# Seven-product output projection of a hybrid block on Trainium2: one order of block products for both row halves, half-sized accumulating loads, and the mixer's signed copies on ScalarE's queue

## The chip, the cores and the metric

The program runs on one core of one Trainium2 chip. The metric is the device time of one execution in microseconds (us), as the median of several runs. The profile is one more execution of the same program, taken by the hardware profiler. Its times are us from the start of its span. PE is TensorE (matmuls; PEld is its weight loads), DVE is VectorE, ACT is ScalarE, POOL is GpSimd, SP is SyncE; a name with a q (ACTq, POOLq, SPq) is the engine's instruction queue where it starts DMAs.

## The reference

One transformer-like block on x of shape (1, 512, 2048) in float32. Two mixers run side by side on one input projection, their outputs are put together and multiplied by `w_out`, and an MLP with a hidden width of 8192 follows.

```python
h = rmsnorm(x, norm_mix_pre)
proj = h @ w_in                                # 2048 -> 1024 (pool) + 4 x 1024 (q, f, i, g)
y_pool = pool_mixer(proj[..., :1024], ...)     # per group: (trailing mean over 2, 4, 8 or 16 rows
                                               #  minus the row) @ pool_w[j] + pool_b[j], times a scale
y_hgrn = hgrn2_mixer(q, f_pre, i, g, ...)      # gated linear recurrence, 8 heads of 128
mix = concat([y_pool, y_hgrn]) @ w_out         # 2048 x 2048
x = x + rmsnorm(mix, norm_mix_post)
h = rmsnorm(x, norm_mlp_pre)
ff = square(relu(h @ w_mlp_in)) @ w_mlp_out    # 2048 -> 8192 -> 2048
x = x + rmsnorm(ff, norm_mlp_post)
```

## The kernel before

**Precision.** Every operand of a large product is kept as two parts, a high part (a cast to a shorter float, on ACT) and a low part (the remainder, a subtraction on DVE). A product is three matmuls on PE: high by high, high by low, low by high. PE therefore carries nearly the whole time, and ACT and DVE feed it with split operands: for each 1 MB of weights (128 x 2048) two casts on ACT (L1052) and two subtractions on DVE (L1053), each of half the block.

**The stages.** The input projection (L269) runs first, column group by column group, until about 542 us. Tasks of other work (the pool mixer, the recurrence) are put between its matmuls by a clock: `clock.tick()` stands after each block of the projection (12 matmuls on one PSUM bank), and a task that says `yield n` is taken up again n ticks later. Then comes the product with `w_out` ("the mix", slots m0 to m27), then the MLP's two products.

**The pool mixer's first half** (`pool_chunk(0)`, c = 0) runs in the second column group. It makes trailing sums on DVE, the difference (`diff`), the split of the difference into `dh` and `dl` (`split`: ACT L514, DVE L515; both live in a tile whose name in the trace is mx), and then `maps(g)`: for each of two output tiles six small matmuls (tile pps, L522 to L524) with the group's weights. There are two groups, g = 0 and 1, which share the rooms `dh` and `dl`.

**The signed copies.** Each mixer's finished 128 x 512 piece goes, with signs + and -, to DRAM (`mix_dram`): `stash` makes two scaled copies on ACT (L465, tile signed, which has two rooms) and starts one 256 KB DMA on POOL's queue (L467). There are 16 of them. The operand sums of the mix are read back from there (tile terms, `load_terms`, and `add_from_dram` L1202, which adds while it loads, on POOL's queue).

**The mix as seven products.** The product with `w_out` is done twice by a seven-product scheme for 2 x 2 blocks, once for each half of the contraction (e = 0, 1), and twice for the pairs of column blocks (n2 = 0, 1): 28 slots of 24 matmuls each (L1132). A slot (n2, i, e) uses product number i, `ORDER = (1, 2, 5, 3, 6, 7, 4)`. Products 1, 6, 7, 4 are summed in the PSUM banks oa, products 2, 5, 3 in the banks og. The weights of products 1, 5, 6, 4 lie in one room (`MXW[n2, e]`) and are made one from the other: when product 1's block has been split, an accumulating DMA on POOL's queue (L1079, 1 MB) adds another block of `w_out` to it in place, and the room holds the weights of product 5; likewise 5 to 6 and 6 to 4. Product 2 has a room of its own (`MY[n2, e]`), which is then loaded anew with the block from which product 3 and, by one accumulating load, product 7 come.

**What sets the order.** For each slot m the program is written in this sequence: the weighing of finished pieces on DVE (`run_weighs`, L1160), the split of slot m+1's weights (`mix_split_gen(m + 1)`, after which the next load or accumulation into that room is issued), the steps that a table `mplan[m]` puts ahead of the slot, the slot's 24 matmuls, and after each half (12 matmuls) the evacuation of its bank (`evac_half`: an ACT copy L1148, or a DVE add L1151 onto the row tile YL) and one clock tick. The second halves of `mplan`'s entries (amid) run after the first half's evacuation. All engines execute their own instructions in this order, so a step that waits holds what stands behind it on its engine. In the order before, the slots for n2 = 0 run through `ORDER` for e = 0 (m0 to m6), and for e = 1 as 2, 1, 5, 3, 6, 7, 4 (m7 to m13). The weights of slot m8 (product 1) go into a room that `late_pools()` opens only at m5 (`second_rooms`), named YZ; its load is an SP DMA.

**Start of the MLP.** Slots k0, k1, ... of a second table, `plan`, are the first MLP products; the steps `s1`, `s2`, `s3`, `s7` make the signed sums of its operand blocks on DVE, `spl` splits them (L913/L914 for weights, similar lines for these).

## Time and profile before

| | |
|---|---|
| time, median of 3 runs | 1947.95 us (1947.37 to 1949.28) |
| the profiled execution's own time | 1949.39 us |
| its span | 1947.7 us |
| mean granted TensorE clock | 0.992 |
| PE busy | 1910.2 us, 10816 matmuls |
| DVE, ACT, POOL busy | 1309.0, 887.3, 186.8 us |
| DMA | 376.61 MB, mean 193 GB/s |

The busy time of PE counts a matmul longer when the clock is granted at less than full speed, so a high share does not say that PE runs at its pace. In a list by time, a row reads: start (us), duration (us), engine, line, operation, out<-in, shape, count, and in brackets the idle time of the engine just before it with what ended that idle time. In a list of waits the columns are: waiting engine, tile and line, the releaser, total us, times, longest. In the table by stretches: the stretch, its length, the busy time of PE, PEld, DVE, ACT, POOL with the number of instructions in brackets, the granted PE clock (PEclk), the DMA share and GB/s.

### The profile page before, as it was taken

To read this page: it belongs to the slowest core of one execution; us is meant where nothing else is said; L and a number is where in the kernel's file an instruction comes from. 1 tells how busy PE (TensorE), PEld (TensorE's weight loads), DVE (VectorE), ACT (ScalarE), POOL (GpSimd) and SP (SyncE) were. 2 spreads that over 40 slices of the span, in tenths; PEclk is the share of its full clock that TensorE was granted. 3 is DMA by queue.
4 is the path that set the end of the run, shared out by engine and by line. 5 is a ranking of instruction groups with operands and counts; after the bars stand their busy time and mean duration, and the time that the engine had idled before them with its cause. 6 is when DMAs were issued, how large, how long until landed. Compare 5 with 4: busy or idle time off the path is not lost.

```text
span 1947.7 us, 26198 instructions
## 1 busy us (share of the span) xinstructions
PE 1910.2 (98%) x10816; PEld 1621.6 (83%) x10816; DVE 1309.0 (67%) x1370; ACT 887.3 (46%) x1063; POOL 186.8 (10%) x291
## 2 busy tenths in 40 slices
PE   9899999999979999999999999999999999999997
PEld 8788888888857899988888888888888888888886
DVE  5537346375557777566665766677778878878787
ACT  6321232213545676444444444446544444444455
POOL 3000000000110101101111111011010010010111
PEclk9999999999989999999999999999999999999999
DMA  8322223323578889988889789898897897897987
GB/s 314 109 87 88 87 92 112 110 88 139 136 204 240 215 232 218 229 235 198 218 218 218 219 217 211 236 236 243 208 248 221 201 236 229 215 222 207 235 215 148
DMA packets 61672, 376.61 MB, mean 193 GB/s; under 512 B 6768, under 2 KB 7792, under 8 KB 23408
## 3 DMA queue, kind: packets, MB, share of 16 engines
q0 software_dynamic: 28064, 176.70, 44.3%
q1 hardware_dynamic: 33344, 197.97, 28.1%
q8 instruction: 85, 1.39, 0.3%
q14 instruction: 35, 0.29, 0.0%
q10 hardware_dynamic: 144, 0.26, 0.0%
HBM read 345.54 MB, written 29.36 MB: 192 GB/s over the span
## 4 chain that ended last, share of the span: by engine, by line
PE 65%; DVE 2%; DMA 1%; ACT 1%; issue 1%; DVEq 0%; ACTq 0%
PE ps L1351 18%; PE al L1571 16%; PE ga L1571 12%; PE ps L1354 9%; PE oa L1132 2%; PE la L1571 2%; PE og L1366 2%; PE lg L1571 2%; PE og L1132 2%; DMA YZ<-in_w_mlp_in 1%; DVE ml L914 1%; PE oa L1366 1%; DVE ml L1053 1%; DMA X<-in_w_out 0%; DMA YZ<-in_w_out 0%
## 5 line engine op out<-in xcount | busy, mean ns | idle before, releaser
L1351 PE MATMUL ps<-a,mh 128*128 128x512 f32 x1536 | 370.6, 391 | 0.0
L1351 PEld LDWEIGHTS ps<-a,mh 128*128 128x128 f32 x1536 | 280.9, 188 | 53.7 <-issue 0.3
L1571 PE MATMUL al<-mh,o 128*128 128x512 f32 x896 | 277.2, 389 | 0.0
L913 ACT CAST mh<-X 128x1024 fp32r<-128x1024 f32 x176 | 180.5, 1055 | 206.4 <-PE ps L1351 82.9
L913 ACT CAST mh<-YX 128x1024 fp32r<-128x1024 f32 x176 | 180.6, 1055 | 159.1 <-PE al L1571 46.3
L914 DVE TENSOR_TENSOR ml<-X,mh 128x1024 fp32r<-128x1024 f32 x176 | 207.4, 1220 | 54.0 <-ACT mh L913 53.8
L269 PE MATMUL pj<-xT,wh 128*128 128x512 f32 x760 | 236.0, 392 | 0.0
L914 DVE TENSOR_TENSOR ml<-YX,mh 128x1024 fp32r<-128x1024 f32 x176 | 207.4, 1220 | 31.3 <-ACT mh L913 31.2
L1571 PE MATMUL ga<-mh,o 128*128 128x512 f32 x672 | 208.0, 389 | 0.0
L1354 PEld LDWEIGHTS ps<-a,ml 128*128 128x128 f32 x1536 | 199.6, 191 | 9.0
L1354 PE MATMUL ps<-a,ml 128*128 128x256 f32 x1536 | 202.4, 283 | 0.0
L1571 PEld LDWEIGHTS al<-mh,o 128*128 128x128 f32 x896 | 168.2, 188 | 35.0
L1571 PE MATMUL al<-ml,o 128*128 128x512 f32 x448 | 174.3, 389 | 0.0
L269 PEld LDWEIGHTS pj<-xT,wh 128*128 128x128 f32 x760 | 142.9, 189 | 29.7
L269 PE MATMUL pj<-wh,xT 128*128 128x512 f32 x512 | 164.7, 395 | 0.0
L228 ACT CAST wh<-wr 128x1024 fp32r<-128x1024 f32 (+1 forms) x84 | 82.5, 1007 | 180.3 <-PE pj L269 142.0
L229 DVE TENSOR_TENSOR wl<-wr,wh 128x1024 fp32r<-128x1024 f32 (+1 forms) x84 | 97.7, 1172 | 94.8 <-ACT wh L228 94.8
L913 ACT CAST mh<-YZ 128x1024 fp32r<-128x1024 f32 x96 | 98.6, 1053 | 127.4 <-PE ps L1351 50.6
L269 PE MATMUL pj<-xT,wl 128*128 128x512 f32 x380 | 148.5, 391 | 0.0
L1571 PEld LDWEIGHTS ga<-mh,o 128*128 128x128 f32 x672 | 126.1, 188 | 26.2
L1400 DVE TENSOR_TENSOR t<-t,ps 128x512 f32<-128x512 f32 x120 | 82.4, 687 | 88.4 <-ACT t L1403 67.2
L914 DVE TENSOR_TENSOR ml<-YZ,mh 128x1024 fp32r<-128x1024 f32 x96 | 113.1, 1220 | 34.4 <-ACT mh L913 34.4
(322 smaller groups left out, 2813.8 us busy)
## 6 DMA issues: line engine op xcount, KB each, us to landing
wr<-in_w_in SPq DMA_DIRECT2D x38, 1024.0 KB, 4.9
X<-in_w_mlp_in POOLq DMA_DIRECT2D x33, 1024.0 KB, 10.0
X<-in_w_mlp_out POOLq DMA_DIRECT2D x33, 1024.0 KB, 8.3
YX<-in_w_mlp_in POOLq DMA_DIRECT2D x23, 1024.0 KB, 9.9
YX<-in_w_mlp_out POOLq DMA_DIRECT2D x23, 1024.0 KB, 9.0
YX<-in_w_mlp_in SPq DMA_DIRECT2D x21, 1024.0 KB, 5.8
YX<-in_w_mlp_out SPq DMA_DIRECT2D x21, 1024.0 KB, 4.8
YZ<-in_w_mlp_in SPq DMA_DIRECT2D x16, 1024.0 KB, 9.0
```

Source lines behind the costliest of these rows:

```text
L228: nc.scalar.copy(out=hi[:, ks, :], in_=raw[:, ks, :])
L229: nc.vector.tensor_tensor(out=lo[:, ks, :], in0=raw[:, ks, :], in1=hi[:, ks, :].bitcast(F32), op=ALU.subtract)
L269: nc.tensor.matmul(bank, l, r, start=first and kt == 0 and oi == 0, stop=last and kt == 3 and oi == 2)
L913: nc.scalar.copy(out=hi[:, ks, :], in_=raw[:, ks, :])
L914: nc.vector.tensor_tensor(out=lo[:, ks, :], in0=raw[:, ks, :], in1=hi[:, ks, :].bitcast(F32), op=ALU.subtract)
L1053: nc.vector.tensor_tensor(out=lo[:, ks, :], in0=halves[h], in1=hi[:, ks, :].bitcast(F32), op=ALU.subtract)
L1132: nc.tensor.matmul(bank[h], l, r[:, kt, :], start=begins and kt == 0 and oi == 0, stop=ends_ and kt == 3 and oi == 2, skip_group_check=True)
L1351: nc.tensor.matmul(o, hi[:, kt, ms], r, start=first and kt == 0, stop=q == 1 and kt == 3 and not first, skip_group_check=True)
L1354: nc.tensor.matmul(o[:, 0], lo[:, kt, ms], r[:, 0], start=False, stop=q == 1 and kt == 3, skip_group_check=True)
L1366: nc.tensor.matmul(o, l[:, kt, ms], r[:, x], start=st and oi == 0 and m % 2 == 0, stop=sp and oi == 2, skip_group_check=True)
L1400: nc.vector.tensor_tensor(out=t, in0=t, in1=half(banks, s_), op=sign)
L1571: nc.tensor.matmul(bank[h] if type(bank) is list else bank[:, h, :], a[:, l, kt, ts], r[:, kt, :], start=i in (1, 2, 5) and kt == 0 and oi ...
```

## The change

Six edits, in the order of the program:

1. `stash` starts its DMA on ACT's queue, not on POOL's.
2. In the pool mixer's task `diff(1)` stands ahead of `maps(0)`. For c = 0 there is one tick more between the first `split` and `maps(0)`, and two ticks instead of one between the second `split` and `maps(1)` (the latter for c = 1 too).
3. The slots of n2 = 0, e = 1 run in `ORDER` like those of e = 0, so product 1 is m7 and product 2 is m8. Room X[1], loaded early by `begin_mix(1)`, takes the weights of product 1; product 2's get a room V (tile MY1), loaded at m3 (`early_y`). `late_pools()` and the loads behind it move from ahead of m5 to within m7 (`second_rooms`), where YZ takes product 3's block, (2, 2); the load of the weighing gain `wpost` for n2 = 0 goes there too (it was at m6). `load_terms(1, 6, 7)` stays at m5, `add_from_dram(7)` goes from m5 to m6, and at m6 the operand of product 1 is split ahead of that of product 2.
4. The accumulating loads of n2 = 0 are issued by halves (512 KB each), each half as soon as that half has been split. For n2 = 1 they stay whole or as they were.
5. For the second problem of n2 = 0 the square sum is taken after product 1's piece is final, which is now product 2's evacuation.
6. At the MLP's start `s2` writes its sum into another block, `s3` and the split for product 6 read it from there, and `s7(1)` and the split for product 4 (from k5, k6 to k9, k10) stand later.

```diff
@@ stash
-        nc.gpsimd.dma_start(mix_dram[c, q]..., sg)
+        nc.scalar.dma_start(mix_dram[c, q]..., sg)
@@ pool_chunk.task
-            if c == 0:
+            else:
                 mixed_room("12a")
+            diff(1, *ws[1])
+            yield 1
             yield from maps(0)
-            diff(1, *ws[1])
             split(1, hi2, ws[1][1])
-            yield 1
+            yield 2
             yield from maps(1)
@@
-    mslots = [(0, i, 0) for i in ORDER] + [(0, i, 1) for i in (2, 1) + ORDER[2:]]
+    mslots = [(0, i, e) for e in range(2) for i in ORDER]
@@ mix_split_gen
+        more = {1: (1, 2), 5: (2, 2), 6: (2, 1), 3: (1, 2)}.get(i)
         for h in range(2):
...
             if h == 0:
                 yield
-        more = {1: (1, 2), 5: (2, 2), 6: (2, 1), 3: (1, 2)}.get(i)
-        if more:
-            load_mix(raw, n2, *more, e, True)
...
-            nxt = {(4, 0): (MXW, (1, 0), X[0], 1), (7, 1): (MXW, (1, 1), X[1], 1),
-                   (4, 1): (MY, (1, 0), YZ.get(0), 2)}.get((i, e)) if n2 == 0 else None
+            if n2 == 0 and more:
+                add_mix(halves[h], n2, *more, e, h)
+        if n2 == 0:
+            nxt = {(4, 0): (MXW, (1, 0), X[0], 1), (4, 1): (MXW, (1, 1), X.get(1), 1),
+                   (7, 1): (MY, (1, 0), YZ.get(0), 2)}.get((i, e))
...
+    def add_mix(dst, n2, a, b, e, h):
+        ks = slice(0, 4) if h is None else slice(2 * h, 2 * h + 2)
+        nc.gpsimd.dma_start(dst, mix_block(n2, a, b, e)[:, ks], accum_op=ALU.add)
@@ begin_mix(1)
-            MY[0, 1] = X[1]
-            load_mix(X[1], 0, 2, 1, 1)
+            MXW[0, 1] = X[1]
+            load_mix(X[1], 0, 1, 1, 1)
@@ evac_half
-        if (n2, e) == (0, 0) or (second and i not in (1, 6, 7, 4)):
+        if (n2, e) == (0, 0) or (second and i not in (2, 6, 7, 4)):
@@
     def second_rooms():
         late_pools()
-        load_terms(1, 6, 7)
-        MXW[0, 1] = YZ[0]
-        load_mix(YZ[0], 0, 1, 1, 1)
+        MY[0, 1] = YZ[0]
+        load_mix(YZ[0], 0, 2, 2, 1)
+        load_wpost(0)
     def second_terms():
         mixed_room("12b")
+        split_plain(1)
         split_plain(2)
-        split_plain(1)
-        load_wpost(0)
+
+    def early_y():
+        MY[0, 1] = hgp.tile([P, 4, 512], F32, tag="V", name="MY1")
+        load_mix(MY[0, 1], 0, 2, 1, 1)
@@ mplan
-        3: ([sum_step(0, 6, 0)], []),
+        3: ([sum_step(0, 6, 0), early_y], []),
-        5: ([second_rooms, lambda: split_plain(4), lambda: add_from_dram(5, 0, 1), lambda: add_from_dram(7, 0, 0)], []),
-        6: ([second_terms], []),
-        7: ([add_step(6, 5)], []),
+        5: ([lambda: load_terms(1, 6, 7), lambda: split_plain(4), lambda: add_from_dram(5, 0, 1)], []),
+        6: ([second_terms, lambda: add_from_dram(7, 0, 0)], []),
+        7: ([add_step(6, 5)], [second_rooms]),
@@ plan, the MLP's start
     def s2(q):
-        return acc((2, 2), (1, 1), ALU.add, q)
+        return lambda: nc.vector.tensor_tensor(out=raw_in(2, 1, q), in0=raw_in(2, 2, q), in1=raw_in(1, 1, q),
+                                               op=ALU.add)
     def s3(q):
-        return acc((1, 2), (2, 2), ALU.subtract, q)
+        return acc((1, 2), (2, 1), ALU.subtract, q)
...
-        5: ([..., s1(1), lambda: new_act(5), spl(5, 0, 2, 1), lambda: new_act(4, yp, "Y"), spl(4, 0, 2, 2)], []),
-        6: ([spl(5, 1, 2, 1), s2(0), spl(4, 1, 2, 2)], []),
+        5: ([..., s7(1), lambda: new_act(5), spl(5, 0, 2, 1), s1(1)], []),
+        6: ([spl(5, 1, 2, 1), s2(0)], []),
-        9: ([lambda: new_act(6), spl(6, 0, 2, 2, True)], []),
-        10: ([spl(6, 1, 2, 2, True)], [keep_pm]),
+        9: ([lambda: new_act(6), spl(6, 0, 2, 1, True), lambda: new_act(4, yp, "Y"), spl(4, 0, 2, 2)], []),
+        10: ([spl(6, 1, 2, 1, True), spl(4, 1, 2, 2)], [keep_pm]),
```

What stands in a row on PE at the pool mixer's first maps, about 60 us into the program, is first the order before: the projection's matmuls (tile pj) and then at once the maps (tile pps).

```order
L269 MATMUL pj_3_566<-xT_187,wh_499 128x512 x2
L269 MATMUL pj_3_566<-xT_187,wl_500 128x512
L522 MATMUL pps<-mx_588,ps_587 128x512
L523 MATMUL pps<-mx_588,ps_587 128x512
L524 MATMUL pps<-mx_588,ps_587 128x512
```

Now the first block of the next weights (bank pj_0, four times these two rows, 12 matmuls) stands ahead of them:

```order
L269 MATMUL pj_3_566<-xT_187,wh_499 128x512 x2
L269 MATMUL pj_3_566<-xT_187,wl_500 128x512
L269 MATMUL pj_0_563<-xT_188,wh_579 128x512 x2
L269 MATMUL pj_0_563<-xT_188,wl_580 128x512
...
L522 MATMUL pps<-mx_588,ps_587 128x512
L523 MATMUL pps<-mx_588,ps_587 128x512
L524 MATMUL pps<-mx_588,ps_587 128x512
```

The maps have moved one block of 12 projection matmuls down; the second group's maps have moved likewise.

On ACT, around slots m5 to m8, the casts of weights (mh), the splits of operands (mx, mx12b, ring, read from terms) and the evacuations (YL<-oa) stood in this order before:

```order
L1052 CAST mh_3807<-X_3760 128x1024 x2
L1004 ACTIVATE mx_588<-terms_3869 128x1024
L1052 CAST mh_3857<-X_3829 128x1024 x2
L1008 CAST mx12b<-terms_3869 128x1024
L1004 ACTIVATE mx12b<-terms_3869 128x1024
L1148 COPY YL<-oa_3859 128x512
L1148 COPY YL<-oa_3860 128x512
L1052 CAST mh_3807<-YZ_4138 128x1024 x2
L1052 CAST mh_3857<-YZ_4138 128x1024 x2
L1008 CAST ring_4137<-terms_3869 128x1024
```

They now stand in this order:

```order
L1054 CAST mh_3807<-X_3760 128x1024 x2
L1005 ACTIVATE mx_588<-terms_3870 128x1024
L1054 CAST mh_3858<-X_3830 128x1024 x2
L1005 ACTIVATE mx12b<-terms_3870 128x1024
L1009 CAST mx12b<-terms_3870 128x1024
L1155 COPY YL<-oa_3860 128x512
L1155 COPY YL<-oa_3861 128x512
L1054 CAST mh_3807<-MY_4034 128x1024 x2
L1054 CAST mh_3858<-X_3830 128x1024 x2
L1009 CAST ring_4230<-terms_3870 128x1024
```

The operand of product 1 (the ACTIVATE of mx12b) has come ahead of that of product 2. Slot m8's weights now come from MY_4034 (the early load), and slot m9's from X_3830 (product 1's room after its accumulation), where both came from YZ_4138, the late room.

On POOL's queue the accumulating loads and the signed copies stood in this order before:

```order
L1079 DMA X_3760<-in_w_out 128x2048 x2
L1079 DMA MY<-in_w_out 128x2048
L1079 DMA X_3760<-in_w_out 128x2048
L467 DMA mix_dram<-signed 128x2x256 x4
L1202 DMA terms_3869<-mix_dram 128x1024 x2
L1079 DMA YZ_4138<-in_w_out 128x2048 x2
```

They now stand in this order:

```order
L1082 DMA X_3760<-in_w_out 128x1024 x4
L1082 DMA MY<-in_w_out 128x1024 x2
L1082 DMA X_3760<-in_w_out 128x1024 x2
L1209 DMA terms_3870<-mix_dram 128x1024
L1082 DMA X_3830<-in_w_out 128x1024 x2
L1209 DMA terms_3870<-mix_dram 128x1024
L1082 DMA X_3830<-in_w_out 128x1024 x2
```

The four signed copies have left this queue for ACT's, each load is in two parts, and the first accumulation of the second problem (X_3830) has come between the two terms.

## The prediction

> **What bounds the kernel now.** I read the page's first rows, PE's list of waits, a table by stretches over the places that the diff touches, and then those places by time.

> ```profile
> PE 1910.2 (98%) x10816; PEld 1621.6 (83%) x10816; DVE 1309.0 (67%) x1370; ACT 887.3 (46%) x1063; POOL 186.8 (10%) x291
> PE og L1132 <- ACT ring L1008: 7.4, 1, 7.4
> PE oa L1132 <- DVE YL L1151: 5.3, 3, 3.6
> PE pps L522 <- ACT mx L514: 4.2, 2, 2.7
> PE oa L1366 <- DVE ml L914: 1.7, 5, 0.8
> 60.80:83.00 22.20, 16.74 (x57) 12.31 (x57) 12.45 (x16) 6.64 (x12) 1.68 (x2) 0.85 0.34 118
> 542.85:607.34 64.49, 50.31 (x192) 39.18 (x193) 44.04 (x49) 27.99 (x39) 5.61 (x7) 0.87 0.79 216
> 607.34:680.00 72.66, 71.64 (x317) 59.02 (x318) 52.63 (x59) 44.23 (x59) 7.19 (x9) 1.00 0.90 232
> ```

> PE bounds the program: 1910.2 of a span of 1947.7 us. The matmuls are the same in number after the change, so all that can go is PE's idle time and its slowed time. The list of waits puts the large ones at three places: the mix (L1132), the pool mixer's maps (L522), the MLP's start (L1366). In the first two of the three rows by stretches the clock is below 1 (0.85, 0.87); in the third PE hardly idles.

> PE by time in the mix, m6 to m13:

> ```profile
> 546.41 0.76 PE L1132 MATMUL oa<-mh,mx 128*128 128x512 f32 x1 [3.57 <-DVE YL L1151]
> 554.60 0.39 PE L1132 MATMUL og<-mh,mx12b 128*128 128x512 f32 x1
> 560.04 0.39 PE L1132 MATMUL oa<-mh,mx12b 128*128 128x512 f32 x1
> 573.23 0.80 PE L1132 MATMUL og<-mh,ring 128*128 128x512 f32 x1 [7.44 <-ACT ring L1008]
> 583.27 0.47 PE L1132 MATMUL og<-mh,ring 128*128 128x512 f32 x1 [1.04 <-DVE YL L1151]
> 595.98 0.47 PE L1132 MATMUL oa<-mh,ring 128*128 128x512 f32 x1 [1.55 <-DVE YL L1151]
> ```

> Slot m7 runs from 554.60 to 560.04: 5.44 us for 24 matmuls, 0.2267 each. That is the full pace. Slot m6, after a wait of 3.57, takes 554.60 - 546.41 = 8.19: the slowed clock costs 2.75 more. Slot m9 takes 583.27 - 1.04 - 573.23 = 9.0, some 3.5 too long. At full pace the 192 matmuls of the stretch are 43.5 of 64.49 us: **21.0 us are lost here**, 13.6 of them in the four waits shown. The 57 matmuls of the pool stretch are 12.9 of 22.20: **9.3 us are lost there**.

> **The pool mixer (edit 2).**

> ```profile
> 60.84 0.39 PE L269 MATMUL pj<-xT,wl 128*128 128x512 f32 x1
> 63.97 0.80 PE L522 MATMUL pps<-mx,ps 128*128 128x512 f32 x1 [2.74 <-ACT mx L514]
> 65.23 0.80 PE L523 MATMUL pps<-mx,ps 128*128 128x512 f32 x1 [0.46 <-DVE mx L515]
> 80.33 0.49 PE L522 MATMUL pps<-mx,ps 128*128 128x512 f32 x1 [1.49 <-ACT mx L514]
> 81.58 0.50 PE L523 MATMUL pps<-mx,ps 128*128 128x512 f32 x1 [0.76 <-DVE mx L515]
> 62.87 1.04 ACT L514 CAST mx<-pa 128x1024 fp32r<-128x1024 f32 x1 [7.66 <-DVE pa L502]
> 63.95 1.23 DVE L515 TENSOR_TENSOR mx<-pa,mx 128x1024 fp32r<-128x1024 f32 x1 [1.17 <-ACT mx L514]
> ```

> The high part is ready at 62.87 + 1.04 = 63.9, the low part at 65.2, whatever PE does. One block of 12 matmuls (2.7 us) now stands ahead of the maps: from 61.2 to 63.95. PE then waits about 1.1 us for the low part instead of 2.74 + 0.46 with the slowed clock behind. The second pair (waits 1.49 + 0.76) gets another block and a `diff` that is made earlier, so both parts should be there. I take 9.3 - 1.1 = **8.2 us**. Bounds: 9.3 if nothing waits, and 5.5 if the remaining wait still slows the clock (2.75 less again). The cover is the projection, which does not depend on the maps.

> **The signed copies (edit 1).**

> ```profile
> 539.63 0.48 ACT L465 ACTIVATE signed<-ops,neg_hnw 128x256 f32<-128x256 f32 x1 [4.88 <-DMA mix_dram<-signed]
> 541.08 2.01 ACT L1052 CAST mh<-X 128x1024 fp32r<-128x1024 f32 x2
> 530.24 0.83 POOL L1079 DMA_DIRECT2D X<-in_w_out  x1 [5.65 <-DVE ml L1053]
> 530.77 1.79 POOL L467 DMA_DIRECT2D mix_dram<-signed  x2
> mix_dram<-signed POOLq DMA_DIRECT2D x16, 256.0 KB, 2.9
> 1941.94 0.37 ACTq L1649 DMA_DIRECT2D out<-YT  x1
> ```

> The 3.57 us before m6 begin on ACT: the third signed copy waits 4.88 us for a room, because a 256 KB copy started at 530.77 on POOL's queue, right behind a 1 MB accumulation (530.24), frees it only at 539.63, after 8.9 us, where the median copy takes 2.9. The cast for m6 (541.08) is late by it, and so are DVE's subtraction and the evacuation behind that, for which PE waits. On a queue of its own the copy should take something between 2.9 and 8.9; nearest are the other copies, so I take ACT's wait as gone. What is late next is the accumulation into X itself and the last recurrence tile, and I leave 1.2 us of wait at m6. ACT issues 16 DMAs more, by the only such row on ACT 0.37 us each, 5.9 in all; 12 of them lie in the projection, on an engine that is busy 46% of the span. The last four (1.5 us) stand between the casts for m4 to m6 and are in the 1.2. POOL loses 16 issues; none of its work waits for anything else by that.

> [...]

> **The order of the mix (edits 3 and 4).**

> ```profile
> 551.17 1.06 ACT L1004 ACTIVATE mx12b<-terms 128x1024 fp32r<-128x1024 f32 x1 [4.30 <-DMA terms<-mix_dram]
> 570.24 1.99 ACT L1052 CAST mh<-YZ 128x1024 fp32r<-128x1024 f32 x2 [10.34 <-DMA YZ<-in_w_out]
> 572.14 1.04 ACT L1008 CAST ring<-terms 128x1024 fp32r<-128x1024 f32 x1
> 561.88 0.84 POOL L1079 DMA_DIRECT2D YZ<-in_w_out  x1 [5.75 <-DVE ml L1053]
> 575.87 1.28 DVE L1151 TENSOR_TENSOR YL<-YL,oa 128x512 f32<-128x512 f32 x2
> 579.03 2.36 DVE L1053 TENSOR_TENSOR ml<-X,mh 128x1024 fp32r<-128x1024 f32 x2 [0.25 <-ACT mh L1052]
> 582.44 1.28 DVE L1151 TENSOR_TENSOR YL<-YL,og 128x512 f32<-128x512 f32 x2
> ```

> The 7.44 us before m9 are one chain: product 1's weights came late in the late room, its accumulation went out at 561.88 and freed ACT at 570.24 (8.4 us), and the cast of the ring tile stands behind that on ACT. Now product 1's room is loaded long before, its first half is accumulated from about m6, and product 2 stands between, so product 5's block has one slot (5.44) and m7's own wait more. I keep 1.1 us there. The slots of the new order, wait by wait:
> - m7: product 1 now follows m6 directly. Its operand needs the term whose DMA held ACT until 551.17; I estimate 549.3 for it (2 us earlier, as ACT and SP are), the split after it 552, and m6's end 549.5: 2.5 us. PE may be slowed by it. Waits of 1.04 and 1.55 did not slow it (560.04 shows the full pace too) and 2.74 did, so I count half of 2.75: 1.4.
> - m10: between two evacuations DVE has two adds, two weighings, two subtractions (2.36 of 579.03) and a ring split: 582.44 - 575.87 = 6.6 us against 5.44 for a slot; that alone is 1.5, near the 1.55 of 595.98. The weighing needs `wpost`, for which see below; for it I double this to 3.0.
> - m12 to m14: 0.7 in all for the same chain, about half of the 1.55 that m12 shows before.

> With m6's 1.2 and m9's 1.1 this is 9.9 us, so 21.0 - 9.9 = **11.1 us** are gained. Bounds: at best only the DVE waits and one more remain (3.2), 17.8; at worst m6 stays as it is (3.57 + 2.75 - 1.2 = 5.1 more) and m7 is slowed in full (1.4 more): 4.6.

> [...]

> The half loads, and `wpost`:

> ```profile
> 643.40 0.84 POOL L1079 DMA_DIRECT2D my<-in_w_out  x1 [5.07 <-DVE ml L1053]
> 644.53 0.85 POOL L1079 DMA_DIRECT2D my<-in_w_out  x1 [0.29 <-DVE ml L1053]
> my<-in_w_out POOLq DMA_DIRECT2D x2, 512.0 KB, 9.1
> X<-in_w_out POOLq DMA_DIRECT2D x2, 1024.0 KB, 11.1
> X<-in_w_out POOLq DMA_DIRECT2D x10, 1024.0 KB, 8.8
> wpost<-in_norm_mix_post SPq DMA_DIRECT2D x2, 512.0 KB, 14.9
> ```

> The program has such a pair already: two halves issued 1.13 us apart, landing 9.1 after issue, where whole blocks beside them took 11.1. A pair so costs no more than a block, and the first half starts a subtraction (1.2 us) earlier. Seven POOL issues more, 0.85 each, lie on an engine that is busy 5.61 of 64.49 us. `late_pools()` opens in the place of the pool that holds MY1, so the load into the late room and that of `wpost` may start only when product 2's block has been split, by my estimate at 556.5 (two casts and two subtractions, 4.4 us, after the 552 of m7). The first weighing, behind m8's evacuation, is due near 565, 8.5 us later. `wpost` took 14.9 us before, with 2 MB started just ahead of it, and a 512 KB half takes 9.1: so something between no wait and 6 us, and DVE's split for m10 stands behind it. Edit 5 only follows the new order (one square per half on ACT, as before).

> **The MLP's start (edit 6).** Of the 1.7 us of L1366 and the waits beside it I take 1.2 off and add 0.5 at k10 for the moved split: **0.7**, between 0 and 1.5. The bodies of the steps are as long as before.

> **Sum.** 8.2 + 11.1 + 0.7 = 20.0 us. The profiled execution (1949.39, 1.7 over its span) would fall to 1929.4; the median shown is 1.44 lower, so it falls from 1947.95 to about **1928.0**.

> **The rivals.**
> A. The DMA engines are full. The stretch has a share of 0.79 of 64.49 us, 51 us of work, which would have to fit in about 52: the accumulations come late. Against it, the stretch behind runs at 0.90 with 72.66 - 71.64 = 1.0 us of PE idle. Four steps 2 us late and one slowing of 2.75 are about 10: 1938.
> B. The signed copies land no sooner on ACT's queue, and m6 keeps 3.57 + 2.75 in place of 1.2: 5.1 more, 1933.1.
> C. Slower: each half costs as much as a whole. A pair then takes twice the 8.8 or so of a block, 17.6 us, against two slots (10.9) until the room is needed. Each of the six steps of the accumulating chain waits 7 us more and is slowed (2.75): some 60 us, so 1947.95 - 20 + 60, near 1988. It decides from about 3.3 us of delay a step (6 x 3.3 = 20). Against it are the rows of 643.40 and 644.53.
> D. The waits nearly all vanish: 9.3 + 17.8 + 1.5 = 28.6, 1919.3.
> E. `wpost` takes its 14.9 again and lands at 571.4, and the weighing and the subtractions (3.8 us) behind it end at 575.2, where m10 could begin at 569.4: 5.8 of wait and 2.75 of slowing instead of 3.0, so 5.5 more: 1933.5. Against it, one `wpost` is loaded, not two, and less is started ahead of it.

> **How the numbers follow.** A change under 0.2% (3.9 us) cannot be told from none here. Forecast (1922 to 1932) 0.56, A 0.12, E 0.12, B 0.07, D 0.06, C 0.05, no change 0.02 (the edits pay in one place and are lost in another). The range goes from D's 1919 to 1937, a little under A and the sum of the low bounds (5.5 + 4.6 + 0 = 10.1, 1937.8); it leaves out C, no change and half of A. Faster has 0.56 + 0.12 + 0.12 + 0.07 + 0.06 = 0.93, same 0.02, slower 0.05.

> **What would show it.** Pool: the first map waits about 1 us and that stretch's clock is near 1. Copies: no wait of ACT at L465 for its DMA, and m6's wait under 1.5. Order: m9's 7.44 is at most 2, m7 shows a new wait of 2 to 3 on the split of product 1's operand. Loads: halves land within 10 us. The forecast fails if POOL's accumulations land over 12 us after issue, if DVE waits on `wpost` for over 3 us, or if a wait over 2.7 us is left anywhere before 607.

## The result and the profile after

The median fell from 1947.66 us to 1929.85 us (1928.93 to 1932.0, 4 runs). The ratio is 0.9909, with a 95% interval of 0.9892 to 0.9926. The forecast of 1928.0 is a ratio of 0.9898. The profiled execution took 1930.43 us and its span 1928.7, so 19.0 us of span went, where the sum had 20.0. Lines have moved: L1132 of before is L1139 now, L1151 is L1158, L1052 is L1054, L1366 is L1377.

The first row of the page, the longest rows of PE's list of waits, and two rows of the table by stretches (PE, PEld, DVE, ACT and POOL busy, then the granted clock, the DMA share, GB/s). The second stretch is the one that before was 542.85 to 607.34: from the end of m5 to the start of m14, 192 matmuls.

```profile
PE 1903.2 (99%) x10816; PEld 1618.3 (84%) x10816; DVE 1308.6 (68%) x1370; ACT 888.1 (46%) x1063; POOL 184.0 (10%) x283
PE oa L1139 <- DVE YL L1158: 3.9, 3, 3.4
PE fps L977 <- ACT RU L982: 1.8, 1, 1.8
PE oa L1377 <- ACT mh L914: 1.7, 1, 1.7
PE og L1139 <- DVE YL L1158: 1.4, 1, 1.4
60.80:83.00 22.20, 22.20 (x98) 18.06 (x97) 14.15 (x18) 9.89 (x18) 0.00 (x0) 1.00 0.33 118
533.92:586.82 52.90, 46.52 (x192) 36.75 (x193) 43.81 (x49) 28.06 (x39) 9.09 (x11) 0.97 0.92 238
```

The pool stretch has no idle time left, at a clock of 1.00. In the mix the same 192 matmuls take 52.90 us instead of 64.49: 11.6 us gained and 9.4 still lost over the 43.5 of the full pace. The DMA share there rose from 0.79 to 0.92. The waits in it, PE by time:

```profile
537.36 0.47 PE L1139 MATMUL oa<-mh,mx 128*128 128x512 f32 x1 [3.44 <-DVE YL L1158]
544.83 0.50 PE L1139 MATMUL oa<-mh,mx12b 128*128 128x512 f32 x1
557.00 0.47 PE L1139 MATMUL og<-mh,ring 128*128 128x512 f32 x1 [0.97 <-issue]
564.09 0.47 PE L1139 MATMUL og<-mh,ring 128*128 128x512 f32 x1 [1.40 <-DVE YL L1158]
575.51 0.47 PE L1139 MATMUL oa<-mh,ring 128*128 128x512 f32 x1 [0.28 <-DVE YL L1158]
586.82 0.47 PE L1139 MATMUL oa<-mh,mx12a 128*128 128x512 f32 x1 [0.16 <-DVE YL L1158]
```

m6 waits as before (3.44 against 3.57), m7 (544.83) does not wait at all, and m9's 7.44 has become 0.97. The chain that ended last, in this part, says why m6 has not moved (start, length, what):

```profile
522.50 8.12 DMA mix_dram<-signed
...
536.02 6.20 DMA terms<-mix_dram
...
549.10 9.46 DMA wpost<-in_norm_mix_post
...
562.51 8.71 DMA YZ<-in_w_out
```

In this piece of the chain, m6 to m13, four transfers follow one another: a signed copy, a term, `wpost`, an accumulation. The first of them holds ACT, in ACT's rows by time:

```profile
522.50 0.37 ACTq L467 DMA_DIRECT2D mix_dram<-signed  x1
530.70 0.47 ACT L465 ACTIVATE signed<-ops,neg_hnw 128x256 f32<-128x256 f32 x1 [4.12 <-DMA mix_dram<-signed]
542.30 1.06 ACT L1005 ACTIVATE mx12b<-terms 128x1024 fp32r<-128x1024 f32 x1 [5.43 <-DMA terms<-mix_dram]
```

The copy was started at 522.50 on ACT's own queue and freed its room 8.1 us later, against 8.9 on POOL's queue before. It ran beside two half accumulations that POOL had started at 520.14 and 521.28. The half accumulations into X land like this (count, KB, median us):

```profile
X<-in_w_out POOLq DMA_DIRECT2D x4, 512.0 KB, 9.4
```

At the MLP's start, PE by time, two rows of before, then two rows of now and a table row of now:

```profile
714.26 2.84 PE L976 MATMUL fps<-ident,YR 128*128 128x128 f32 x16 [0.81 <-ACT RU L981]
749.28 0.69 PE L1366 MATMUL oa<-a,mh 128*128 128x256 f32 x2 [0.50 <-ACT mh L913]
694.76 2.84 PE L977 MATMUL fps<-ident,YR 128*128 128x128 f32 x16 [1.83 <-ACT RU L982]
729.27 0.70 PE L1377 MATMUL oa<-a,mh 128*128 128x256 f32 x2 [1.68 <-ACT mh L914]
732.00:735.80 3.80, 3.80 (x20) 3.80 (x21) 3.80 (x4) 3.80 (x6) 0.86 (x1) 0.55 0.56 73
```

The transposes at 694.76 wait 1.0 us longer than at 714.26 before. The small waits between the two rows of before (0.16, 0.51, 0.16 and 0.50) are one wait of 1.68, yet the way from the first row to the second is 34.51 us where it was 35.02. Soon after it the clock is at 0.55 for a stretch in which before it was 1.00. Of the 20.5 us gained at m14 (607.34 to 586.82), 19.0 arrive at the end.

### The profile page after: what moved, and what is told of

Read it like the earlier page. It is cut to its first block, busy times and chain, and to the rows that moved or that the text cites. A ratio compares the mean times of both kernels' runs of the same rounds, so it can differ in the third digit from the quotient of the medians.

```text
span 1928.7 us, 26203 instructions
## 1 busy us (share of the span) xinstructions
PE 1903.2 (99%) x10816; PEld 1618.3 (84%) x10816; DVE 1308.6 (68%) x1370; ACT 888.1 (46%) x1063; POOL 184.0 (10%) x283
## 3 DMA queue, kind: packets, MB, share of 16 engines
q1 hardware_dynamic: 33344, 197.97, 28.6%
## 4 chain that ended last, share of the span: by engine, by line
PE 95%; DMA 2%; DVE 1%; ACT 1%; issue 1%; SPq 0%; POOL 0%; DVEq 0%; ACTq 0%; POOLq 0%
PE pj L269 23%; PE ps L1362 18%; PE al L1582 16%; PE ga L1582 12%; PE ps L1365 10%; PE oa L1139 3%; PE og L1139 3%; PE og L1377 2%; PE la L1582 2%; PE lg L1582 2%; PE oa L1377 2%; PE lps L659 1%; PE pm L1377 1%; DMA wpost<-in_norm_mix_post 0%; DMA YZ<-in_w_out 0%
## 5 line engine op out<-in xcount | busy, mean ns | idle before, releaser
L914 ACT CAST mh<-X 128x1024 fp32r<-128x1024 f32 x176 | 180.6, 1056 | 205.7 <-PE ps L1362 82.9
L914 ACT CAST mh<-YX 128x1024 fp32r<-128x1024 f32 x176 | 180.7, 1056 | 158.9 <-PE al L1582 46.3
L269 PE MATMUL pj<-xT,wh 128*128 128x512 f32 x760 | 234.8, 390 | 0.0
L269 PEld LDWEIGHTS pj<-xT,wh 128*128 128x128 f32 x760 | 142.1, 188 | 29.3
L269 PE MATMUL pj<-wh,xT 128*128 128x512 f32 x512 | 164.8, 395 | 0.0
L914 ACT CAST mh<-YZ 128x1024 fp32r<-128x1024 f32 x96 | 98.6, 1054 | 128.9 <-PE ps L1362 51.1
L269 PE MATMUL pj<-xT,wl 128*128 128x512 f32 x380 | 148.1, 390 | 0.0
## 6 DMA issues: line engine op xcount, KB each, us to landing
wr<-in_w_in SPq DMA_DIRECT2D x38, 1024.0 KB, 4.8
X<-in_w_mlp_in POOLq DMA_DIRECT2D x33, 1024.0 KB, 9.6
X<-in_w_mlp_out POOLq DMA_DIRECT2D x33, 1024.0 KB, 8.4
YX<-in_w_mlp_in POOLq DMA_DIRECT2D x23, 1024.0 KB, 9.9
YX<-in_w_mlp_out POOLq DMA_DIRECT2D x23, 1024.0 KB, 8.9
YX<-in_w_mlp_in SPq DMA_DIRECT2D x21, 1024.0 KB, 5.9
YX<-in_w_mlp_out SPq DMA_DIRECT2D x21, 1024.0 KB, 4.9
YZ<-in_w_mlp_in SPq DMA_DIRECT2D x16, 1024.0 KB, 8.4
```

The source lines that it names most:

```text
L269: nc.tensor.matmul(bank, l, r, start=first and kt == 0 and oi == 0, stop=last and kt == 3 and oi == 2)
L914: nc.scalar.copy(out=hi[:, ks, :], in_=raw[:, ks, :])
```

## The experiments

Experiments 1 to 4, 5 to 8 and 9 to 11 are three groups, each on one chip together with the kernel before; the ratio is to the kernel before in that group (medians of 1949.04, 1947.81 and 1948.46 us), with its 95% interval. The changed kernel itself was not in these groups, so a comparison with its 1929.85 goes from one group to another.

**1. The pool mixer alone** (the kernel before, with edit 2).

```diff
+            diff(1, *ws[1])
+            yield 1
             yield from maps(0)
-            diff(1, *ws[1])
             split(1, hi2, ws[1][1])
-            yield 1
+            yield 2
             yield from maps(1)
```

> The kernel before with edit 2 alone (the pool mixer's maps one block later, diff(1) ahead of them). Theory: this edit alone takes away the whole loss of the pool stretch, since one block of the projection covers both parts of the split: the waits of 2.74, 0.46, 1.49 and 0.76 us go and with them the two half-rate windows, 9.3 us in all, so about 1938.5 against 1947.7 (ratio 0.9952), and the mix stays as it was before (waits of 3.57 and 7.44). Rival: the second pair of maps only moves its wait down the line, 5.5 us, 1942.

Measured: 1942.22 (1940.19 to 1943.79), ratio 0.9965 (0.9952 to 0.9979); the profiled span was 1938.5, 9.2 less than before. The table row and the mix's two large waits:

```profile
60.80:83.00 22.20, 22.20 (x99) 18.24 (x98) 14.37 (x19) 9.80 (x18) 2.41 (x3) 1.00 0.31 115
537.85 0.77 PE L1133 MATMUL oa<-mh,mx 128*128 128x512 f32 x1 [4.20 <-DVE YL L1152]
564.47 0.79 PE L1133 MATMUL og<-mh,ring 128*128 128x512 f32 x1 [7.20 <-ACT ring L1009]
```

The stretch's loss is gone whole, and the mix keeps its large waits. The median gives 6.8 us, the profile 9.2; the interval (4 to 9.4 us) holds both. What the old pool mixer loses is itself not constant. Experiment 5 has it unchanged, and there the same stretch reads:

```profile
60.80:83.00 22.20, 17.62 (x73) 13.38 (x73) 12.59 (x17) 7.99 (x16) 2.42 (x3) 1.00 0.29 111
```

The clock did not fall (1.00, against 0.85 in the kernel before), 73 matmuls fit in where the kernel before had 57, and some 5.6 us are lost instead of 9.3. So what edit 2 gains depends on whether the slow clock would have come in that run; the median lies between the two.

**2. The copies back on POOL's queue** (the changed kernel without edit 1).

```diff
-        nc.scalar.dma_start(mix_dram[c, q]..., sg)
+        nc.gpsimd.dma_start(mix_dram[c, q]..., sg)
```

> The changed kernel with edit 1 undone: the signed copies start on POOL's queue again. Theory: ACT's queue brought nothing at m6, because the changed trace still shows a wait of 4.12 us of ACT for a copy that took 8.1 us to land; so the time stays within 2 us of 1929.9, with a wait of 3 to 4 us at m6. Rival: on POOL's queue the copies fall behind two half accumulations and POOL's 0.85 us issues, ACT waits 6 us or more, m6 later by 2 to 4 and slowed longer (6.8 us at half rate instead of 3.4, 1.7 more): 1934 to 1936.

Measured: 1930.39 (1929.3 to 1930.77), ratio 0.9903 (0.989 to 0.9917): the same as the changed kernel. ACT's wait for the copy and m6's wait behind it:

```profile
ACT signed L465 <- DMA mix_dram<-signed: 5.4, 1, 5.4
538.05 0.77 PE L1139 MATMUL oa<-mh,mx 128*128 128x512 f32 x1 [3.86 <-DVE YL L1158]
```

ACT waits 1.3 us longer (5.4 against 4.12) and PE 0.4 (3.86 against 3.44). Edit 1 is worth nothing that the runs can tell: 1929.85 us on ACT's queue and 1930.39 us on POOL's.

**3. Whole accumulating loads** (the changed kernel without edit 4).

```diff
-            if n2 == 0 and more:
-                add_mix(halves[h], n2, *more, e, h)
+        if n2 == 0 and more:
+            add_mix(raw, n2, *more, e, None)
```

> The changed kernel with edit 4 undone: the accumulating loads of n2 = 0 go out whole, after the second half's split. Theory: a pair of halves lands as early as a whole that is issued with the first half, so without it each accumulation is 1.2 us later at its first half and lands in about 8.5 us; at m9, m11 and m6, where ACT waits for a landing, PE waits 1 to 2 us more each and one more half-rate window (1.7 us) may come: 1932 to 1936. Rival: the order alone did it and halves only add issues: within 1 us of 1929.9 or lower.

Measured: 1934.07 (1933.59 to 1934.97), ratio 0.9924 (0.9911 to 0.9936). All five runs lie above all four of the changed kernel and of experiment 2; by the medians the halves are worth about 4 us. PE by time at m6, m9, m12, and a row of PE's list of waits:

```profile
539.49 0.77 PE L1139 MATMUL oa<-mh,mx 128*128 128x512 f32 x1 [4.34 <-DVE YL L1158]
559.69 0.47 PE L1139 MATMUL og<-mh,ring 128*128 128x512 f32 x1 [1.24 <-issue]
579.18 0.47 PE L1139 MATMUL oa<-mh,ring 128*128 128x512 f32 x1 [1.71 <-DVE YL L1158]
PE pps L523 <- DVE mx L515: 0.8, 1, 0.8
```

m6 waits 0.9 longer, m12 1.4 longer, m9 0.3, and m6's slow clock lasts 6.8 us instead of 3.4. From the start of m0 to that of m14 this profile takes 97.0 us, the changed kernel's 94.5, so 2.5 us are found in the mix. The profile's m0 starts 1.2 us later already, nearly all of it lost by the end of the pool stretch, which the edit does not touch. The last row is from the pool mixer, which this experiment does not touch: here the maps do wait 0.8 for the low part, as the prediction had it (1.1), and in the changed kernel's profile they did not.

**4. The MLP's start as before** (the changed kernel without edit 6; the tables `plan`, `s2`, `s3` of before). Edit 6 also starts one accumulating load of MLP weights two slots later, from k1 to k3, which the list of edits does not name; it is undone here too.

```diff
-        9: ([lambda: new_act(6), spl(6, 0, 2, 1, True), lambda: new_act(4, yp, "Y"), spl(4, 0, 2, 2)], []),
+        9: ([lambda: new_act(6), spl(6, 0, 2, 2, True)], []),
...
```

> The changed kernel with edit 6 undone: the MLP's start as it was before. Theory: edit 6 only moved waits (0.16 + 0.51 + 0.16 + 0.50 + 0.75 of before became 1.68 + 0.75 at one place), and the wait of 1.68 was followed by a half-rate window of 3.4 us that cost 1.7; so undone it is 1 to 2 us faster, about 1928.5. Rival (my prediction's step): edit 6 saves 0.7, so undone it is 0.7 slower, 1930.6.

Measured: 1930.67 (1928.48 to 1932.46), ratio 0.9905 (0.9892 to 0.9919). Neither size can be told apart from no effect. The profile settles the clock, though. PE at the place and the table row behind it:

```profile
731.37 0.70 PE L1376 MATMUL oa<-a,mh 128*128 128x256 f32 x2 [0.52 <-ACT mh L914]
733.00:737.50 4.50, 4.34 (x23) 4.14 (x24) 4.50 (x5) 3.54 (x5) 0.86 (x1) 0.62 0.42 58
```

With the old start and its small waits the clock falls here too. With edit 6, experiments 6 and 10 have the same wait of 1.67 and no slow stretch behind it. So the slow stretch is not the price of edit 6's 1.68, and the theory of the expectation falls. What the traces do show is 0.5 us: from the transposes to this row it is 35.0 us in the four profiles with the old start, and 34.5 in the changed kernel and in every experiment with edit 6 in which the clock did not fall on the way.

**5. The order alone** (the kernel before, with edits 3 and 5).

```diff
-    mslots = [(0, i, 0) for i in ORDER] + [(0, i, 1) for i in (2, 1) + ORDER[2:]]
+    mslots = [(0, i, e) for e in range(2) for i in ORDER]
...
```

> The kernel before with edits 3 and 5 alone: the order of the slots and of their loads as in the changed kernel, but whole accumulating loads, the pool mixer, the signed copies and the MLP's start as before. Theory: the order removes m9's wait (7.2 us to about 1) and its half-rate windows, but m6 keeps its wait of about 4 and its windows; that is 11.5 us of the mix less the 3.7 that the half loads give, some 7 us: 1941.5 against 1949 (ratio 0.996). Rival: the halves made the order work; without them m9's wait stays above 3 and the gain is under 3 us.

Measured: 1939.0 (1936.97 to 1940.06), ratio 0.9952 (0.9939 to 0.9964), 8.8 us by the medians. PE at m6 and m9:

```profile
543.00 0.47 PE L1138 MATMUL oa<-mh,mx 128*128 128x512 f32 x1 [3.92 <-DVE YL L1157]
563.46 0.47 PE L1138 MATMUL og<-mh,ring 128*128 128x512 f32 x1 [1.93 <-issue]
```

m9's 7.4 is gone without the halves. The profile's span is 12.3 us shorter than before, but 3.7 of that were gained ahead of the mix, where this run's pool mixer kept its clock (experiment 1). From m0 to m14 it takes 96.7 us against 106.1, so 9.4 is what the order gains in the mix. By the medians: order 8.8, pool mixer 6.8, halves about 4, the other two nothing: 19.6, against 17.8 measured together, within what the intervals allow.

**6. A third room for the signed copies** (the changed kernel and this).

```diff
+        if (c, q, k) == (1, 0, 2):
+            sg = hgp.tile([P, 512], F32, tag="near", name="signed3").rearrange(...)
+        else:
             sg = junk_tile([P, 512], "signed").rearrange("p (t s) -> p t s", t=2)
```

> The changed kernel with a third room for the signed copies: the third of the last four pieces is written to a room that lies free at that time, so ACT need not wait for a copy to land. Theory: ACT's wait of 4.1 us goes; the cast for m6 then waits for the accumulation into X, which lands about 9.4 us after issue, so m6 waits 1.5 to 2 instead of 3.4 to 3.9 and the half-rate window (1.7 us) goes in most runs; but m7's operand, behind X's load on SP's queue, comes hardly sooner, and m7 gets a wait of 1 to 2: together 2 us less than the changed kernel, about 1928 (where it has 1930). Rival: the accumulation is the real limit and m6 waits as long as before: no change, 1930.

Measured: 1928.33 (1926.68 to 1929.63), ratio 0.9897 (0.9882 to 0.9912).

```profile
536.20 0.47 PE L1142 MATMUL oa<-mh,mx 128*128 128x512 f32 x1 [1.43 <-DVE YL L1161]
543.57 0.50 PE L1142 MATMUL oa<-mh,mx12b 128*128 128x512 f32 x1 [1.66 <-ACT YL L1158]
```

m6 waits 1.43 instead of 3.44, near the 1.2 of the prediction, and its clock does not fall. m7 gets the wait that the prediction gave it, 1.66: the releaser is ACT's evacuation, which stands on ACT behind the split of m7's operand. So the room was the cause at m6, and m6's lateness was what hid m7's operand. The time hardly moved (1.5 us by the medians, intervals overlapping); from m0 to m14 the profile is 1.4 us shorter.

**7. The terms' loads first** (the changed kernel, terms 6 and 7 loaded ahead of X[0] on SP's queue).

```diff
-        5: ([lambda: load_terms(1, 6, 7), lambda: split_plain(4), ...
+        5: ([lambda: split_plain(4), ...
...
+        if m == 5:
+            load_terms(1, 6, 7)
         for _ in mix_split_gen(m + 1):
```

> The changed kernel with the loads of terms 6 and 7 put ahead of the load into X[0] on SP's queue (before m5's split steps, not behind them). Theory: m7 does not wait for its operand in the changed kernel, since m6's own wait and slow clock give it the time; so alone this does nothing, within 1 us of 1930. Rival: the term's landing also sets ACT's casts for m8 and m9, so that earlier terms take away m9's 0.7 to 1.0 and part of m10's 0.9 to 1.9: 1 to 2 us faster.

Measured: 1930.65 (1929.65 to 1933.27), ratio 0.9914 (0.99 to 0.9927): nothing. PE at m6 and m10:

```profile
537.76 0.47 PE L1139 MATMUL oa<-mh,mx 128*128 128x512 f32 x1 [3.39 <-DVE YL L1158]
564.45 0.47 PE L1139 MATMUL og<-mh,ring 128*128 128x512 f32 x1 [2.86 <-DVE YL L1158]
```

m6 waited as in the changed kernel, but its clock stayed full, so m6 took 5.54 us instead of 7.47. The 1.9 us so gained were lost again at m9 (1.52) and m10 (2.86), against 0.97 and 1.40; DVE waited 2.65 us for `wpost` ahead of m10. Here, too, an earlier m6 only uncovered the waits behind it.

**8. Third room and terms first.**

> The changed kernel with both: a third room for the signed copies, and the terms' loads ahead of X[0]'s. Theory: with m6 earlier, m7's operand would come last, and the terms ahead of the 1 MB load take that wait away as well: 3 to 4 us less than the changed kernel, about 1926.5. Rival: as with the third room alone (1928), when the terms wait for the last signed copy to land and not for the queue.

Measured: 1929.32 (1928.93 to 1930.44), ratio 0.9906 (0.9892 to 0.9919): no gain over the changed kernel. PE at m6 and m9 (m7 does not wait), then the piece of the chain ahead of m10:

```profile
536.04 0.47 PE L1142 MATMUL oa<-mh,mx 128*128 128x512 f32 x1 [1.10 <-ACT mh L1057]
554.99 0.47 PE L1142 MATMUL og<-mh,ring 128*128 128x512 f32 x1 [2.35 <-issue]
546.17 12.44 DMA wpost<-in_norm_mix_post
```

PE reaches m9 sooner and waits there instead. DVE then waits 3.2 us for `wpost`, which lands at 558.6, as in the changed kernel, though it was started 2.9 us earlier.

**9. The load into X[0] at m9 instead of m5** (the changed kernel; 1 MB less among the transfers of m6 to m9).

```diff
-            nxt = {(4, 0): (MXW, (1, 0), X[0], 1), (4, 1): ...
+            nxt = {(4, 1): ...
...
+        if m == 9:
+            MXW[1, 0] = X[0]
+            load_mix(X[0], 1, 1, 1, 0)
```

> The changed kernel with the 1 MB load into X[0] (weights of slot m14) put off from m5 to m9. Theory: the DMA engines are full from 536 to 557, and without this megabyte the terms and the accumulations land 1 to 2 us earlier; but m6's wait of 3.4 lies ahead of it and stays, and behind it only m9's 0.7 to 1.0 can go: 1929, at most 1 us less than the changed kernel. Rival: the load at m9 then delays the accumulations for m11 to m13, and m12's or m14's wait grows by 1 to 2: 1931.

Measured: 1929.93 (1929.27 to 1933.56), ratio 0.9906 (0.9891 to 0.9922): nothing by itself. m10's wait fell from 1.40 to 0.90 and m12's rose from 0.28 to 1.20, about as the rival had it.

**10. Third room, terms first, and X[0] at m9.**

> Third room, terms first, and X[0]'s load at m9. With room and terms alone the time fell hardly below the changed kernel's: m9 waited 2.35 us and m10 1.87. Theory: m9's 2.35 is the accumulation and the added term landing late among full DMA engines (9.6 and 11.9 us); without the megabyte they land sooner and m9 waits under 1.2, so 1 to 2 us are gained: 1927.5 to 1928.5. Rival: DVE's weighing behind wpost's landing (12.4 us after its start) sets m10 whatever m9 does; m9's wait moves to m10 (3 or more) and the time stays at 1929.3.

Measured: 1926.91 (1924.7 to 1928.08), ratio 0.9886 (0.9871 to 0.99). Its four runs all lie below the four of experiment 9, on the same chip. PE at m6, m9 and m10, then the landings from 533 to 565 (count, KB, median us):

```profile
536.06 0.47 PE L1142 MATMUL oa<-mh,mx 128*128 128x512 f32 x1 [1.68 <-DVE YL L1161]
553.28 0.47 PE L1142 MATMUL og<-mh,ring 128*128 128x512 f32 x1 [0.66 <-issue]
559.91 0.47 PE L1142 MATMUL og<-mh,ring 128*128 128x512 f32 x1 [0.94 <-DVE YL L1161]
X<-in_w_out POOLq DMA_DIRECT2D x5, 512.0 KB, 8.3
terms<-mix_dram POOLq DMA_DIRECT2D x2, 512.0 KB, 7.5
```

With the megabyte out of the way the accumulations land in 8.3 us (9.6 in experiment 8) and the added terms in 7.5 (11.9), and m9's wait falls from 2.35 to 0.66. So the transfers did bound m9 once m6 was early. DVE does not wait for `wpost` here. This is the fastest kernel of the study by its median, some 3 us below the changed one; against the changed kernel's own interval the two just overlap.

**11. As 10, with `wpost` ahead of the load into the late room.**

```diff
-        load_mix(YZ[0], 0, 2, 2, 1)
         load_wpost(0)
+        load_mix(YZ[0], 0, 2, 2, 1)
```

> As the last, and wpost's load ahead of the 1 MB load into the late room (YZ) on SP's queue. Theory: DVE's weighing no longer waits, m10's wait falls from nearly 2 to under 1; 1 to 2 us less than the last: about 1926.5. Rival: both loads share the same engines, so that YZ's block (m10's weights) lands as much later as wpost comes earlier, and m10 waits for the cast instead: no change.

Measured: 1927.37 (1925.98 to 1928.95), ratio 0.9887 (0.9871 to 0.9904): no change, as the rival had it. In experiment 10 the weighing had already stopped waiting for `wpost`, so the theory had nothing left to take. m10 waits 2.29 here:

```profile
560.41 0.47 PE L1142 MATMUL og<-mh,ring 128*128 128x512 f32 x1 [2.29 <-DVE YL L1161]
YZ<-in_w_out SPq DMA_DIRECT2D x1, 1024.0 KB, 9.7
```

The block of 1 MB now lands in 9.7 us where it took 6.0 in experiment 10, and ACT's cast for m10 waits 1.27 us for it.

## Why the prediction was right, and where its steps were not

The time was 1.85 us above the forecast and inside its range. Two of the three terms were close, but one of them by errors that cancelled, which is luck. Of the prediction's own signs, the pool stretch's clock, m9's wait and the landing of the halves (9.4 us) came; ACT's wait for the copy did not go, m6's wait stayed over 1.5 and m7 got no wait. One sign of failure came too: a wait over 2.7 us before 607 was left, m6's 3.44.

- **Pool mixer, 8.2.** The profiles have 9.3 (8.96 by the start of m0, 501.24 to 492.28, and 0.34 that the changed run was behind at the last block ahead of the maps). That is the upper bound: the maps found both parts ready. Experiment 3's wait of 0.8 shows the remaining wait of the prediction in a run that began a little otherwise. It did not slow the clock. The 9.3 that the prediction started from is one profile's loss; experiment 5's profile lost 5.6 with the same pool mixer.
- **Mix, 11.1; measured 11.6.** Slot by slot: m6 was to lose 1.2 and lost 3.44 and then 2.0 over the full pace (7.47 us for the slot), 1.7 of it by the slow clock; m7 was to lose 3.9 and lost nothing; m9 1.1, measured 0.97; m10 3.0, measured 1.40; m12 to m14 0.7, measured 0.44. The failed step is "I take ACT's wait as gone": the copy was to land like the median copy, and it took 8.1 us. Rival B described it and got a chance of 0.07. Its price of 5.1 was near what m6 lost beyond its 1.2 (4.2), but m7's term had to fall with it: the operand that comes late for an early m6 is in time for a late one. Experiment 6 shows both numbers at once. The two should not have been added as if they were independent.
- **`wpost` (rival E).** It landed 9.5 us after its start and DVE waited 1.16 us for it, between the forecast's ends of 0 and 6.
- **MLP's start, +0.7.** Between m14 and the end the changed profile lost 1.5. Experiment 4 says that edit 6 has no effect that the times can tell. In the traces it takes off 0.5 us, near the 0.7; the loss comes from beside it. One part is the transposes' wait (1.83). It is 0.5 to 0.9 in the four profiles with the old start and 0.6 to 2.2 in the nine with edit 6; why it is long in four of these stays open. Another is the half-rate stretch, which came with the old start too. That the small waits became one of 1.68 has a plain reason: PE came early to a chain (squares, row sums, a sum on DVE, a cast, the cast of weights) that starts at its evacuation and takes 8.25 us before (741.03 to 749.28) and after (721.02 to 729.27).
- **Half loads (rival C).** A pair cost no more than a block here: a half landed in 9.4 us (median), a whole block of before in 8.8, and the first PE wait behind it was 0.97, not 7. Experiment 3 gives about 4 us for them by the medians and 2.5 in the mix's trace, which the prediction had inside the 11.1 and did not size alone.
- **Full DMA engines (rival A).** The share rose to 0.92, as the rival reckoned, without the 10 us of lateness. It became a limit at m9 only when the other waits ahead of it were taken away (experiments 8 and 10).

## What to carry to other kernels

When two waits lie on one chain, the first one's delay is the second one's cover: take away the first and the second appears (m6's 3.44 became 1.43 in experiment 6, and m7, which had not waited, waited 1.66), so price them together, and look for gain only where the last of the chain moves too. A transfer that was late among busy DMA engines (a share of 0.90) came hardly sooner from another engine's queue, 8.1 us after its start against 8.9; what took the wait away was a further room for its source, and then less traffic at that time (m9's 2.35 became 0.66). Work whose inputs are just late can be moved behind one block of independent matmuls, which here took away the whole loss of a stretch, 9.3 us. A loss that hangs on the clock is not the same in every run (9.3 and 5.6 us with the same pool mixer): before it is counted as a gain, it should be read in more than one profile.

## What the runs showed of the hardware

**The slow clock came in steps.** In the clock record of these traces the half-rate stretches (granted clock 0.50) in the middle of the program are 3.4, 6.8 or 10.2 us long, never another length: 6.8 at the pool maps and at m6 before, 10.2 behind the 7.44 at m9, 3.4 at m6 after. A step of 3.41 us at half rate cost half of its length, 1.7 us, so the 2.75 that the prediction took from m6 for every slowed place was no constant. In the changed kernel a table row over one such step:

```profile
537.40:541.30 3.90, 3.90 (x10) 3.06 (x11) 2.68 (x3) 0.00 (x0) 2.33 (x3) 0.56 0.95 367
```

The size of a wait alone did not decide: at m6, waits of 3.4 to 4.3 us were followed by one step in some runs, by two in others and by none in experiment 7, and at the MLP's start the clock fell behind waits of 0.52 and 0.76 us in experiment 4 and did not in the kernel before, with waits of 0.50 and 0.75.

**A 256 KB copy took 8 to 9 us beside accumulating loads**: 8.1 on ACT's queue beside two half accumulations in the changed kernel, and 8.9 on POOL's queue right behind a whole one in the kernel before, against a median of 2.9 over the 16 copies before. The DMA share in those 8.1 us was 0.90.
